# A two-layer streaming encoder: the order of work at two stage entries, and the place of one conditioning product

## The chip, the core and the metric

The kernel runs on one core of a Trainium2 chip. The metric is the device time of one execution in microseconds. The core has a matrix engine (TensorE, PE in the rows; PEld is its weight load), VectorE (DVE), ScalarE (ACT), GpSimd (POOL) and a queue engine that issues transfers (SyncE, SP).

## The reference

Two layers work on 1024 prompt tokens and 64 sample tokens at width 1024. Each sub-layer is norm, conditioning, product, gated residual. Cut to what matters:

```python
sc = silu(c)
for l in range(2):
    m = (sc @ w_ada[l] + b_ada[l])              # 6 vectors of 1024 for each token group
    sh1, sc1, g1, sh2, sc2, g2 = (m[:, i] for i in range(6))
    hn = rms_norm(x, norm_mix[l]) * (1 + sc1) + sh1
    o = even_mix(hn, ...) if l % 2 == 0 else odd_mix(hn, ...)
    x = x + (1 + g1) * o
    hn = rms_norm(x, norm_ffn[l]) * (1 + sc2) + sh2
    x = x + (1 + g2) * ((silu(hn @ wg) * (hn @ wu)) @ wd)
y = rms_norm(x, final_norm)
```

`even_mix` is stick-breaking attention beside a gated linear recurrence (HGRN), `odd_mix` a Griffin block whose first step is `hn @ w_in` into a gate half and an x half. `rms_norm` needs the sum of the squares of a token over all 1024 features before the token can be scaled. The vector `g2` of layer 0, called the fifth conditioning here (i = 5), is first needed when the feed-forward of layer 0 adds its result to x.

## The kernel before

Everything is kept with features on the 128 partitions and tokens along the free axis: NT = 1088 tokens, eight tiles `x[k]`. A float32 product is made of three passes: each operand is split into a rounded high part and the rest (`split`, L98: the cast on ACT, the subtraction of L100 on DVE or POOL), and PE adds hi·hi, hi·lo and lo·hi. For most products the tokens go in chunks `CH` of 384, 384 and 320.

The stages follow one another in the span: the first norm and product to 94 us; the even layer to 840 us, in which attention and HGRN interleave with the input projection (`gemm`, L129, its weights loaded by `load_in`, L1080); output projection and second norm to 908 us; `up_half(0)` to 1374 us; `down_half(0)` to 1642 us; the entry of the odd layer, that is its first norm and the products with the first x and gate columns, to 1692 us; the odd layer's loop to 2060 us; `up_half(1)` to 2514 us; `down_half(1)` and the final norm to 2800 us.

What sets the order. A scheduler simulates the engines and orders each engine's instructions by priority: `later()` lowers the priority, `soon()` raises it. The wrappers `oV`, `oS`, `oG` and `oPE` keep their instructions in program order instead; `V`, `S`, `G`, `PE` leave them to the scheduler. Each engine then runs its list strictly in order.

**The conditioning.** A vector of `m` for 128 features needs 1024 products for each of the two token groups. There are two forms. `mods_dve` (L190) multiplies a 128x1024 tile of the transposed weights by silu(c) held in two tiles `cbc`: for each group one DVE instruction that multiplies and accumulates, or, with `shared`, for the second group a POOL multiplication (L193) and an ACT accumulation (L194). The other form runs on PE: `load_in` (L1080) takes, once its 24 DVE units are done, one tile of `ada5` at a time through eight products into a bank and a copy to `mods` (L1096 and L1097). Before, the fifth conditioning of layer 0 is made in this second form, under `later()`, in the even layer.

**The seven-product stage.** `up_half` (L425) forms gate and up products of the feed-forward for 20 blocks f = 2 to 21 with seven products of half size in place of eight. Block f has products into the accumulators X, Y, Z, W, X, Z, W, each with 24 matmuls of 128x272; after each product a use runs: n1, n6, p7, n5, n2, p4, p3. `weights(f)` makes seven split weight tiles (`wh` by ACT, `wl` by POOL) out of four raw ones and of sums on DVE (`s`, `wu`, `wg`). The token operands are made once, in `sums` (L467): ACT adds the shift to eight x tiles, DVE forms 16 differences (L477 to L480), and ACT and DVE split 16 halves into T1 to T4. One untransformed block f = 1 runs ahead of them.

`Ada` (L399) does conditioning in the shadow of these blocks: a unit in n1 (two DVE instructions), one in n5 (shared form), and for f below 8 a third one in n2 (shared form). `up_half(0)` does 40 units of layer 1, `up_half(1)` the eight of the gate of layer 1. `load_cbc` (L183) makes the tiles `cbc` by a sigmoid on ACT and a product on DVE (L187).

**The odd entry.** `down_half(0)` calls `after(ci)` when the tokens of chunk ci are final. `use` (L1205) there runs `stats(ci)` for chunks 0 and 1: `norm_stats` (L251) squares the eight x slices (ACT), adds them (DVE), sums over partitions on PE, takes the power on POOL (L234) and spreads it on PE (L241); then `norm_apply` (L267) scales (DVE), shifts (ACT) and splits (ACT, and POOL for five of eight tiles, DVE for three) into h. `stats(2)` is called after the products of chunk 0 (24 matmuls with `wx0`, 24 with `wg0`) with all its PE steps in program order.

## Time and profile before

| | us |
|---|---|
| median of 3 runs | 2803.64 (2800.59 to 2804.72) |
| the profiled execution | 2801.73 |
| its span | 2800.0 |
| PE busy in the span | 2616.5 |
| DVE, ACT, POOL busy | 1855.6, 1022.0, 1180.6 |
| mean granted clock of PE | 0.963 of full |

The profiled execution is 1.73 us longer than its span and 1.91 us under the median. PE is the engine that works most; time in which PE waits, or runs at the lower of its two clock levels (0.5 of full), is what a change of order can touch. A row of the windows view gives a stretch, its length, the busy time and number of instructions of PE, PEld, DVE, ACT and POOL, the granted clock, the share of the DMA engines and the GB/s. A row of the timeline gives a start, a duration, engine, line and operation, output and inputs, size and count, and in brackets the idle time before it and what ended that.

### The profile page before, as it was taken

The numbers are of one execution on the slowest core, as the hardware profiler recorded it, in microseconds if no ns is written. First come the engines' busy times: TensorE is split into PE (matmuls) and PEld (weight loads), VectorE is DVE, ScalarE is ACT, GpSimd is POOL, SyncE is SP. The second block draws the span as 40 slices with busy tenths as digits, with TensorE's granted clock in tenths as the row PEclk, the third lists the DMA queues.
The fourth block names the chain that finished last, engine by engine and source line by source line (L and its number), as shares of the span: only waits on it lengthen the run. The fifth ranks groups of instructions, "written<-read, shape, count | busy, mean of one in ns | idle before, by whom it ended". The sixth has DMA issues, their size and how long they took to land. (4 is left out here: it accounts for less than half of the span.)

```text
span 2800.0 us, 44597 instructions
## 1 busy us (share of the span) xinstructions
PE 2616.5 (93%) x17680; PEld 2553.8 (91%) x17680; DVE 1855.6 (66%) x2850; ACT 1022.0 (36%) x1862; POOL 1180.6 (42%) x795
## 2 busy tenths in 40 slices
PE   5898999999988899999999979998889999999998
PEld 5898989998878899999999979988889999999997
DVE  8768763667897778876465575658877444446556
ACT  3225343354454533333221146564363222222112
POOL 6446443455441477765322233444126444433112
PEclk8999989899999999999999989999999999999999
DMA  6232111113112344443432101121223222226211
GB/s 240 91 113 92 46 58 55 57 53 130 57 50 103 108 141 133 130 138 108 152 130 94 62 16 59 68 74 63 98 74 122 70 81 83 70 92 219 89 61 64
DMA packets 99663, 261.98 MB, mean 94 GB/s; under 512 B 16640, under 2 KB 36096, under 8 KB 99456
## 3 DMA queue, kind: packets, MB, share of 16 engines
q1 hardware_dynamic: 99168, 258.03, 27.7%
q8 instruction: 139, 2.28, 0.3%
q10 hardware_dynamic: 288, 1.11, 0.1%
q14 instruction: 68, 0.56, 0.1%
HBM read 208.41 MB, written 50.69 MB: 93 GB/s over the span
## 5 line engine op out<-in xcount | busy, mean ns | idle before, releaser
L100 POOL TENSOR_TENSOR w_lo<-w_raw,w_hi 128x1024 fp32r<-128x1024 f32 x92 | 237.3, 2586 | 533.9 <-ACT w_hi L99 484.6
L100 POOL TENSOR_TENSOR wl<-wg,wh 128x512 fp32r<-128x512 f32 x164 | 225.4, 1381 | 375.6 <-ACT wh L99 333.6
L507 PE MATMUL accZ<-op,wh 128*128 128x272 f32 x1280 | 245.5, 289 | 5.8 <-DVE tmp L51 5.7
L507 PE MATMUL accW<-op,wh 128*128 128x272 f32 x1280 | 244.3, 288 | 0.0
L507 PE MATMUL accX<-op,wh 128*128 128x272 f32 x1280 | 243.5, 288 | 0.0
L99 ACT CAST w_hi<-w_raw 128x1024 fp32r<-128x1024 f32 x90 | 93.2, 1050 | 362.3 <-PE ps_mm L313 253.5
L129 PE MATMUL ps_mm<-h_hi,w_hi 128*128 128x384 f32 (+1 forms) x624 | 213.2, 342 | 2.8 <-ACT w_hi L99 1.3
L129 PE MATMUL ps_mm<-h_hi,w_lo 128*128 128x384 f32 (+1 forms) x624 | 212.4, 342 | 2.0 <-POOL w_lo L100 2.0
L129 PE MATMUL ps_mm<-h_lo,w_hi 128*128 128x384 f32 (+1 forms) x624 | 212.0, 340 | 0.0
L507 PEld LDWEIGHTS accZ<-op,wh 128*128 128x128 f32 x1280 | 201.1, 188 | 7.6 <-DVE tmp L51 6.2
L99 ACT CAST wh<-wg 128x512 fp32r<-128x512 f32 x160 | 97.5, 619 | 296.9 <-DVE wg L51 191.4
L318 DVE SCALAR_TENSOR_TENSOR x<-ps_mm,mods,x 128x384 f32<-128x384 f32 (+4 forms) x334 | 152.2, 480 | 75.1 <-PE ps_mm L313 73.9
L507 PEld LDWEIGHTS accW<-op,wh 128*128 128x128 f32 x1280 | 201.3, 188 | 0.0
L507 PEld LDWEIGHTS accX<-op,wh 128*128 128x128 f32 x1280 | 200.9, 188 | 0.0
L507 PE MATMUL accZ<-op,wl 128*128 128x272 f32 x640 | 184.6, 288 | 1.0 <-POOL wl L100 1.0
L507 PE MATMUL accX<-op,wl 128*128 128x272 f32 x640 | 184.5, 288 | 0.0
L507 PE MATMUL accW<-op,wl 128*128 128x272 f32 x640 | 184.5, 288 | 0.0
L318 DVE SCALAR_TENSOR_TENSOR x<-ps_t,mods,x 128x384 f32<-128x384 f32 (+3 forms) x220 | 107.1, 504 | 87.9 <-PE ps_t L313 87.9
L51 DVE SCALAR_TENSOR_TENSOR tmp<-hid,cbc 128x1024 f32<-128x1024 f32 x68 | 132.0, 1941 | 21.6 <-ACT tmp L194 20.9
L100 POOL TENSOR_TENSOR wl<-wu,wh 128x512 fp32r<-128x512 f32 x84 | 131.7, 1569 | 27.9 <-ACT wh L99 27.3
L507 PE MATMUL accY<-op,wh 128*128 128x272 f32 x640 | 124.7, 292 | 16.1 <-ACT wh L99 16.1
L318 DVE SCALAR_TENSOR_TENSOR x<-ps_z,mods,x 128x384 f32<-128x384 f32 (+2 forms) x198 | 91.3, 485 | 61.4 <-PE ps_z L313 60.6
(485 smaller groups left out, 8066.1 us busy)
## 6 DMA issues: line engine op xcount, KB each, us to landing
hid<-in_adaT SPq DMA_DIRECT2D x48, 512.0 KB, 3.9
w_raw<-in_wd SPq DMA_DIRECT2D x44, 512.0 KB, 3.8
hid_dram<-tmp SPq DMA_DIRECT2D x80, 272.0 KB, 2.1
hid_lo<-hid_dram SPq DMA_DIRECT2D x40, 544.0 KB, 4.7
wg<-in_wg SPq DMA_DIRECT2D x42, 512.0 KB, 3.9
wu<-in_wu SPq DMA_DIRECT2D x42, 512.0 KB, 3.6
w_raw<-in_w_in_even SPq DMA_DIRECT2D x28, 512.0 KB, 3.7
w_raw<-in_adaT SPq DMA_DIRECT2D x24, 512.0 KB, 3.6
```

The lines of the kernel that those rows point to most:

```text
L51: return lambda *a, **k: self.tc.keep_in_program_order(f(*a, **k))
L99: S.copy(hi, src)
L100: (lo_eng or G).tensor_sub(lo, src, hi.bitcast(F32))
L129: PE.matmul(ps[:, :n], a[:, k * P:(k + 1) * P], b[:, c0:c0 + n], start=(i == 0), stop=(i == last))
L318: V.scalar_tensor_tensor(x[m][:, r0:r0 + rn], ps[:, r0 - c0:r0 - c0 + rn], gate[:, m, b:b + 1], x[m][:, r0:r0 + rn], ALU.mult, ALU.add)
L507: PE.matmul(acc[:, j, :Q], a[:, k * P:(k + 1) * P], op[k][:, b, c], start=(start == 1 and i == 0), stop=(i == 11), skip_group_check=True)
```

## The change

Four edits.

1. **Odd entry.** `norm_stats` is split into `norm_squares` (squares and their sum) and the rest. `after(ci)` makes the squares of chunk ci ahead of the scaling of chunk ci-1, the squares of chunk 2 ahead of the scaling of chunk 1. The sum of chunk 2 over partitions and the power come after the 48 products of chunk 0, its spread and scaling after the first 24 of chunk 1.
2. **The fifth conditioning.** The PE form in `load_in` is gone with its 64 calls, its eight loads of `ada5` and its copies. `Ada` of `up_half(0)` gets 48 units in place of 40, and the blocks with a third unit are f = 2 to 15 in place of f = 2 to 7; in `up_half(1)` no block has a third unit, where f = 2 to 4 had one.
3. **`load_cbc`** uses silu on ACT alone; the sigmoid and the two DVE products of L187 go, and with the function the changes between two ACT tables.
4. **`sums`** adds the shift in the order 0, 4, 1, 5, 2, 6, 3, 7, does 12 of the 16 differences first, then the splits in the order of the products that use them (T2, T3, T1, T4), and keeps all of it in program order.

```diff
...
-    def load_cbc(ts, sg):
+    def load_cbc(ts):
         for v in range(2):
             dma(ts[v], I["cT2"][v:v + 1, :].partition_broadcast(P))
-            S.activation(sg, ts[v], AF.Sigmoid)
-            V.tensor_mul(ts[v], ts[v], sg)
+            S.activation(ts[v], ts[v], AF.Silu)
         return ts
...
     def norm_stats(chunk, x, tmp, PE=PE, pool=(1, 2), S=S):
+        acc = norm_squares(chunk, x, tmp, pool, S)
+        return inv_rms([lambda: acc], chunk[1], 1.0 / 1024, PE)
+
+    def norm_squares(chunk, x, tmp, pool=(), S=S):
...
-        return inv_rms([lambda: acc], n, 1.0 / 1024, PE)
+        return acc
...
         def __init__(self, todo):
-            self.todo = [(i, j) for i in todo for j in range(KD)]
+            self.todo = [(l, i, j) for l, i in todo for j in range(KD)]
+            self.thrice = 2 + max(0, len(self.todo) - 2 * (FF - 5))
...
-            self.cb = load_cbc([pool.tile([P, 1024], F32, name="cbc", tag="cbc", bufs=2) for v in range(2)],
-                               raw())
+            self.cb = load_cbc([pool.tile([P, 1024], F32, name="cbc", tag="cbc", bufs=2) for v in range(2)])
...
-                dma(raw, I["adaT"][48 + i * KD + j])
...
-                mods_dve(1, i * KD + j, self.cb, raw, self.junk, shared, oV)
+                l, i, j, raw = self.ready.pop(0)
+                mods_dve(l, i * KD + j, self.cb, raw, self.junk, shared, oV)
                 if j == KD - 1:
-                    finish_mods(1, i)
+                    finish_mods(l, i)
     def up_half(l, plain, x, t_tag, op_tag, ada):
         B = B12, B11, B21, B22 = plain[0]
...
             def sums():
-                for k in range(KD):
+                for k in (0, 4, 1, 5, 2, 6, 3, 7):
                     for r0, rn, b in rng(0, NT):
                         v = x[k][:, r0:r0 + rn]
                         oS.activation(v, v, AF.Identity, bias=mods[l][:, 3 * KD + k, b:b + 1])
                 T1, T3, T4 = ([halves(fp.tile([P, NT], F32R, name="op", tag=t, bufs=4)) for _ in range(4)]
                               for t in ("t1", "t3", "t4"))
+                T2 = []
+                part = lambda k: (x[k][:, :HT], x[k][:, HT:], x[k + 4][:, :HT], x[k + 4][:, HT:])
                 for k in range(4):
-                    a, b, c, d = x[k][:, :HT], x[k][:, HT:], x[k + 4][:, :HT], x[k + 4][:, HT:]
-                    V.tensor_sub(d, b, d)
-                    V.tensor_sub(b, b, a)
-                    V.tensor_sub(a, a, d)
-                    V.tensor_sub(c, c, a)
-                    split(d, T3[k][:, 0, :], T3[k][:, 1, :], V, S=oS)
-                    split(b, T1[k][:, 0, :], T1[k][:, 1, :], V, S=oS)
-                    split(c, T4[k][:, 0, :], T4[k][:, 1, :], V, S=oS)
-                T2 = []
+                    a, b, c, d = part(k)
+                    oV.tensor_sub(d, b, d)
+                    oV.tensor_sub(b, b, a)
+                    oV.tensor_sub(a, a, d)
                 for k in range(4):
                     T2.append(halves(u(op_tag, F32R, "op")))
-                    split(x[k][:, :HT], T2[k][:, 0, :], T2[k][:, 1, :], V)
+                    split(part(k)[0], T2[k][:, 0, :], T2[k][:, 1, :], oV, S=oS)
+                for k in range(4):
+                    split(part(k)[3], T3[k][:, 0, :], T3[k][:, 1, :], oV, S=oS)
+                for k in range(4):
+                    split(part(k)[1], T1[k][:, 0, :], T1[k][:, 1, :], oV, S=oS)
+                for k in range(4):
+                    a, b, c, d = part(k)
+                    oV.tensor_sub(c, c, a)
+                    split(c, T4[k][:, 0, :], T4[k][:, 1, :], oV, S=oS)
                 return B11, T2, T3, T1, B21, T4, B22
             stage["open"].close()
...
                     def n2():
                         S.activation(g, x_, AF.Silu)
-                        if f < 8:
+                        if f < ada.thrice:
                             ada.one(True)
                             ada.fetch(1)
...
                 yield
         todo = [(i, j) for i in (2, 3, 4) for j in range(KD)]
-        todo_pe = list(range(KD))
         def load_in(t):
             w = load_w(wi[t])
...
                     mods_dve(0, i * KD + j, cb, raw, lambda: mp.tile([P, 1024], BF16, name="junk", tag="junk"))
                     if j == KD - 1:
                         finish_mods(0, i)
-                if not todo and todo_pe:
-                    j = todo_pe.pop(0)
-                    raw = raw_tile()
-                    dma(raw, I["ada5"][j])
-                    ps = bank("o")
-                    for e in range(KD):
-                        PE.matmul(ps[:, :2], raw[:, e * P:(e + 1) * P], sc[:, e, :], start=(e == 0), stop=(e == KD - 1))
-                    V.tensor_copy(mods[0][:, 5 * KD + j, :], ps[:, :2])
-                    if j == KD - 1:
-                        finish_mods(0, 5)
             return w
         def out_group(g, after=None, chunks=CH):
...
     stage["open"] = banks_open
-    got = up_half(0, plain, x, "B", "A", Ada(range(5)))
+    got = up_half(0, plain, x, "B", "A", Ada([(0, 5)] + [(1, i) for i in range(5)]))
     xg_open = ExitStack()
     xg = xg_open.enter_context(phase_pool("xg"))
...
         ntmp = lambda: fp.tile([P, 384], F32, name="ntmp", tag="ntmp", bufs=13)
         h = []
-        def use(x):
-            rs = {}
-
-            def stats(ci, PE=PE):
-                rs[ci] = norm_stats(CH[ci], x, ntmp, PE, (), oS if ci == 2 else S)
-                if not h:
-                    h.extend(new_h("B", "C"))
-                for k in range(KD):
-                    norm_apply(ci, k, x, rs[ci], 1, 0, h, ntmp)
-
-            use.stats = stats
+        accs, rs = {}, {}
+
+        def squares(ci):
+            accs[ci] = norm_squares(CH[ci], x, ntmp, (), oS if ci == 2 else S)
+
+        def apply(ci):
+            if not h:
+                h.extend(new_h("B", "C"))
+            for k in range(KD):
+                norm_apply(ci, k, x, rs[ci], 1, 0, h, ntmp)
+
+
+        def use(x_):
+            nonlocal x
+            x = x_
             with later():
                 decay_consts()
-            return None, lambda ci: stats(ci) if ci < 2 else None, None
-
-        x = down_half(0, fp, "A", "B", got, use)
+
+            def after(ci):
+                squares(ci)
+                if ci == 0:
+                    rs[0] = inv_rms([lambda: accs[0]], CH[0][1], 1.0 / 1024)
+                elif ci == 1:
+                    apply(0)
+                    rs[1] = inv_rms([lambda: accs[1]], CH[1][1], 1.0 / 1024)
+                else:
+                    apply(1)
+
+            return None, after, None
+
+        down_half(0, fp, "A", "B", got, use)
         wio = I["w_in_odd"]
         OS = 1027
...
         for ci in range(3):
             hold = lambda to: lambda *a: outs.append((to, a))
             gemm_chunk(wx0, h, hold(x_to(xg0, oS)), ci, range(KD), ("mm", "t", "mm")[ci], oPE)
+            if ci == 1:
+                rs[2] = rms_spread(r2, CH[2][1], oPE)
+                apply(2)
             gemm_chunk(wg0, h, hold(g_to(xg0, oS)), ci, range(KD), ("z", "z", "t")[ci], oPE)
             if ci == 0:
-                use.stats(2, oPE)
+                r2 = rms_pow(rms_sum([lambda: accs[2]], CH[2][1], oPE), CH[2][1], 1.0 / 1024)
             with soon():
                 while outs:
                     to, a = outs.pop(0)
...
     xg_open.close()
-    got = up_half(1, plain, x, "A", "B", Ada((5,)))
+    got = up_half(1, plain, x, "A", "B", Ada([(1, 5)]))
     with phase_pool("ffn1") as fp:
         stage["w"] = fp
         layout(fp, ("hid", 2 * NT, 2), ("late", 2 * NT, 1), ("wd_lo", 1024, 6), ("w_raw", 1024, 2),
```

In the lists below, one row is an instruction or several alike: line, operation, output and inputs, tile. L51 stands for all instructions that a wrapper issues in program order; numbers behind a name tell buffers apart.

VectorE at the start of `up_half(0)`, before, up to the weight sum `wg` from which the second product's weights are split (`x` are differences, `op<-x,op` low parts of splits, `hid` the block f = 1, the last row is the first conditioning unit):

```order
L386 TENSOR_TENSOR hid_8640<-hid_8640,accZ 128x272
L100 TENSOR_TENSOR op<-x,op 128x544
L480 TENSOR_TENSOR x<-x 128x544
L100 TENSOR_TENSOR op<-x,op 128x544
L386 TENSOR_TENSOR hid_8640<-hid_8640,accW 128x272
L100 TENSOR_TENSOR op<-x,op 128x544 x2
L51 TENSOR_TENSOR wu<-wg,wu 128x512
L100 TENSOR_TENSOR op<-x,op 128x544 x2
L51 TENSOR_TENSOR wg<-s_8871,wg 128x512
L51 SCALAR_TENSOR_TENSOR tmp,mods_70<-hid_8863,cbc 128x1024 x2
```

The same engine and place after:

```order
L51 TENSOR_TENSOR op<-x,op 128x544 x9
L51 TENSOR_TENSOR x<-x 128x544
L389 TENSOR_TENSOR hid_8542<-hid_8542,accZ 128x272
L389 TENSOR_TENSOR hid_8542<-hid_8542,accW 128x272
L51 TENSOR_TENSOR s_8770<-wu 128x512
L51 TENSOR_TENSOR op<-x,op 128x544
L51 TENSOR_TENSOR x<-x 128x544
L51 TENSOR_TENSOR wu<-wg,wu 128x512
L51 TENSOR_TENSOR wg<-s_8770,wg 128x512
L51 SCALAR_TENSOR_TENSOR tmp,mods_69<-hid_8762,cbc 128x1024
```

Of the 16 differences 14 and of the 16 low parts 13 stand ahead of `wg` now, where all 32 did; three of the low parts and two differences come behind it, and the two products of L187 are gone.

VectorE in block f = 8 of `up_half(0)`, before (`tmp,mods` is a conditioning unit, `tmp<-accZ,tmp` at the sixth product the sum that frees Z):

```order
L51 TENSOR_TENSOR tmp<-accW,tmp 128x544
L51 SCALAR_TENSOR_TENSOR tmp,mods_70<-hid_10239,cbc 128x1024
L51 TENSOR_TENSOR s_10428<-wu 128x512
L51 TENSOR_TENSOR wu<-wg,wu 128x512
L51 TENSOR_TENSOR wg<-s_10428,wg 128x512
L51 TENSOR_TENSOR tmp<-accZ,tmp 128x544
L51 TENSOR_TENSOR tmp<-tmp 128x544
```

The same block after:

```order
L51 TENSOR_TENSOR tmp<-accW,tmp 128x544
L51 SCALAR_TENSOR_TENSOR tmp,mods_70<-hid_10138,cbc 128x1024
L51 TENSOR_TENSOR s_10327<-wu 128x512
L51 TENSOR_TENSOR wu<-wg,wu 128x512
L51 TENSOR_TENSOR wg<-s_10327,wg 128x512
L51 SCALAR_TENSOR_TENSOR tmp,mods_70<-hid_10238,cbc 128x1024
L51 TENSOR_TENSOR tmp<-accZ,tmp 128x544
L51 TENSOR_TENSOR tmp<-tmp 128x544
```

A third unit stands between the weight sum and the sum that frees Z, as it stood in blocks 2 to 7 before.

TensorE in the odd entry, before, at the end of chunk 0's products (`ones,ntmp` is the sum of squares over partitions, `ident,r` the spread, `ps_t` the first products of chunk 1):

```order
L51 MATMUL ps_z<-h_hi,w_hi 128x384
L225 MATMUL ps_o<-ones,ntmp 128x1 x3
L51 MATMUL ps_z<-h_lo,w_hi 128x384
L51 MATMUL ps_z<-h_hi,w_lo 128x384
L51 MATMUL ps_z<-h_hi,w_hi 128x384
L51 MATMUL ps_z<-h_lo,w_hi 128x384
L51 MATMUL ps_z<-h_hi,w_lo 128x384
L241 MATMUL ps_o<-ident,r_15861 128x128 x3
L51 MATMUL ps_o<-ones,ntmp 128x1 x3
L51 MATMUL ps_o<-ident,r_16067 128x128 x3
L51 MATMUL ps_t<-h_hi,w_hi 128x384
```

The sum of chunk 2 after, behind the last of chunk 0's products:

```order
L51 MATMUL ps_z<-h_hi,w_hi 128x384
L51 MATMUL ps_z<-h_lo,w_hi 128x384
L51 MATMUL ps_z<-h_hi,w_lo 128x384
L51 MATMUL ps_o<-ones,ntmp 128x1 x3
L51 MATMUL ps_t<-h_hi,w_hi 128x384
L51 MATMUL ps_t<-h_lo,w_hi 128x384
```

and the spread of chunk 2 after, between the x and the gate products of chunk 1:

```order
L51 MATMUL ps_t<-h_hi,w_hi 128x384
L51 MATMUL ps_t<-h_lo,w_hi 128x384
L51 MATMUL ps_t<-h_hi,w_lo 128x384
L51 MATMUL ps_o<-ident,r_16008 128x128 x3
L51 MATMUL ps_z<-h_hi,w_hi 128x384
L51 MATMUL ps_z<-h_lo,w_hi 128x384
```

The sum and the spread of chunk 2 stood next to each other ahead of all products of chunk 1; now 24 products of chunk 1 stand between them. The sum of chunk 1, which stood 43 products into chunk 0, stands in the last products of `down_half(0)`, and its spread 19 products into chunk 0.

## Rows read from the trace of the kernel before

**Rows 1.** The page: busy us, share of the span and instructions of each engine

```profile
PE 2616.5 (93%) x17680; PEld 2553.8 (91%) x17680; DVE 1855.6 (66%) x2850; ACT 1022.0 (36%) x1862; POOL 1180.6 (42%) x795
```

**Rows 2.** Windows, line 1096 alone: us, PE busy (x), PEld busy (x), clock, DMA share, GB/s

```profile
392.00:409.50 17.50, 6.91 (x32) 7.29 (x32) 0.51 0.31 99
409.50:438.00 28.50, 3.74 (x32) 3.96 (x32) 1.00 0.10 31
492.00:508.50 16.50, 2.93 (x13) 3.12 (x13) 0.50 0.38 121
340.00:560.00 220.00, 20.03 (x128) 21.04 (x128) 0.88 0.18 56
```

**Rows 3.** Timeline of PE in the even layer: start, us, instruction

```profile
395.63 3.51 PE L1096 MATMUL ps_o<-sc,w_raw 128*128 128x2 f32 x16
399.01 1.52 PE L904 MATMUL ps_t<-ident,be 128*128 128x128 f32 x6
```

**Rows 4.** Waits of PE, 340 to 560 us: us in total, times, longest

```profile
PE ps_t L904 <- DVE vs L855: 2.5, 1, 2.5
```

**Rows 5.** Windows at the start of up_half(0), all engines

```profile
936.40:944.70 8.30, 0.35 (x4) 0.13 (x2) 8.30 (x14) 3.54 (x8) 0.02 (x1) 0.83 0.45 148
944.70:948.70 4.00, 4.00 (x16) 3.88 (x17) 2.58 (x4) 1.98 (x4) 4.00 (x3) 0.50 0.42 116
```

**Rows 6.** Timelines of ACT and DVE at the same place

```profile
910.30 8.83 ACT L51 ACTIVATE x<-x,mods 128x1024 f32<-128x1024 f32 x13
943.99 0.62 ACT L99 CAST wh<-wg 128x512 fp32r<-128x512 f32 x1 [4.08 <-DVE wg L51]
916.83 0.72 DVE L477 TENSOR_TENSOR x<-x 128x544 f32<-128x544 f32 x1 [9.09 <-ACT x L51]
926.68 1.22 DVE L187 TENSOR_TENSOR cbc<-cbc,hid 128x1024 f32<-128x1024 f32 x1
943.28 0.68 DVE L51 TENSOR_TENSOR wg<-s,wg 128x512 f32<-128x512 f32 x1
```

**Rows 7.** Timeline of PE at the start of up_half(1)

```profile
2091.68 0.82 PE L507 MATMUL accY<-op,wh 128*128 128x272 f32 x2 [7.95 <-ACT wh L99]
```

**Rows 8.** Windows of blocks: f = 4, f = 5, f = 5 to 8, f = 9; up_half(1) f = 5

```profile
985.88:1006.93 21.05, 21.05 (x171) 21.05 (x170) 14.58 (x16) 7.88 (x15) 16.07 (x9) 1.00 0.47 152
1006.93:1030.68 23.75, 22.06 (x171) 21.30 (x169) 20.49 (x23) 6.75 (x13) 17.07 (x9) 1.00 0.41 136
1006.93:1098.51 91.58, 86.51 (x675) 84.81 (x674) 76.08 (x81) 29.89 (x55) 67.43 (x36) 1.00 0.44 140
1110.53:1131.58 21.05, 21.05 (x171) 21.05 (x169) 19.00 (x19) 7.62 (x14) 14.92 (x10) 1.00 0.50 150
2153.83:2176.68 22.85, 21.88 (x171) 21.23 (x169) 13.12 (x18) 7.17 (x13) 14.12 (x10) 1.00 0.23 78
```

**Rows 9.** Timelines of DVE and POOL, third units of f = 3 and f = 7, and between

```profile
987.03 2.10 DVE L51 SCALAR_TENSOR_TENSOR tmp<-hid,cbc 128x1024 f32<-128x1024 f32 x1 [2.26 <-ACT tmp L194]
1079.08 2.11 DVE L51 SCALAR_TENSOR_TENSOR tmp<-hid,cbc 128x1024 f32<-128x1024 f32 x1 [2.26 <-ACT tmp L194]
1007.86 0.69 DVE L51 TENSOR_TENSOR wu<-wg,wu 128x512 f32<-128x512 f32 x1
1050.24 2.71 DVE L51 TENSOR_TENSOR wu<-wg,wu 128x512 f32<-128x512 f32 x1
1049.68 2.72 POOL L193 TENSOR_TENSOR hid<-hid,cbc 128x1024 f32<-128x1024 f32 x1 [1.23 <-issue]
```

**Rows 10.** Windows of the odd entry

```profile
1657.90:1670.50 12.60, 0.03 (x1) 0.00 (x0) 12.36 (x17) 8.07 (x18) 6.99 (x6) 0.67 0.00 0
1670.50:1679.20 8.70, 7.41 (x27) 7.35 (x28) 4.40 (x16) 3.73 (x12) 2.59 (x3) 0.50 0.00 0
```

**Rows 11.** Timelines of PE and POOL there

```profile
1670.55 1.41 PE L51 MATMUL ps_o<-ones,ntmp 128*128 128x1 f32 x6 [12.62 <-DVE ntmp L263]
1663.02 6.11 POOL L100 TENSOR_TENSOR h_lo<-ntmp,h_hi 128x384 fp32r<-128x384 f32 x5 [0.43 <-ACT h_hi L99]
```

7 lines of the change are left out of this document (3 added, 4 removed).

## The prediction

> **What bounds the kernel now.** I read the totals first: PE is busy 93% of the span, no other engine over 66% [rows 1]. So time goes down where PE has less to do, waits less or runs at full clock, and it goes up where an edit makes PE wait. Then, stage by stage, the windows and the waits of PE in the four places that the diff touches. In the even layer PE is nearly gapless, but a part of what it does is the fifth conditioning, 128 tiny matmuls, partly at half clock [rows 2]. At the start of each `up_half` PE stands still for some 8 us and runs 4 us at half clock behind it [rows 5, 7]. In blocks 5 to 8 of `up_half(0)` it waits for the DVE sum that frees accumulator Z, and blocks with two units run without a gap [rows 8]. In the odd entry it stands still for 12.6 us and then runs at half clock for 8.7 us [rows 10, 11].
>
> **a) The fifth conditioning leaves PE.** The trace has 128 matmuls of line 1096, 20.0 us of busy time in all: 32 take 6.91 us and 13 take 2.93 us at half clock (0.22 us each), 32 take 3.74 us at full clock (0.12 us each) [rows 2]. A run of them overlaps what follows it by 0.13 us (395.63 + 3.51 against 399.01 [rows 3]); with some ten runs that is 1.3 us, so 18.7 us of PE's time go. Is that on the path? PE's longest wait in the stretch is 2.5 us [rows 4], so the stage is bound by PE, with waits that some of these matmuls may cover. The stretches around them are the ones at half clock, 17.5 and 16.5 us long [rows 2]: there PE's work is thin, 128x2 outputs among it, and the scheduler of the new kernel has projection matmuls of 128x384 to put in these places. If a fifth of the 34 us at half clock came back to full, that is 34 x 0.2 / 2 = 3.4 us more. I take -22. Upper end: all but the half of them covered waits, -8. Lower end: half of the 34 us comes back, 8.5, and with the ordering a little better, -34. The eight loads move from the even layer to `up_half(0)`, where the DMA engines are busy 0.50 of a block at most [rows 8]; cost nothing. The eight copies of L1097 were on a DVE with slack.
>
> **b) Start of up_half(0).** PE waits 936.4 to 944.7 for the weights of the second product: the wait is for ACT's cast at 943.99, that for DVE's `wg` at 943.28, and DVE has worked off its list without a gap since 916.83 [rows 5, 6]. Ahead of `wg` stood 40 instructions. In the new list 2 differences and 3 low parts come behind it, 5 x 0.64 = 3.2 us, and the two products of L187 are gone, 2 x 1.2 = 2.4 us [rows 6]: 5.6 us. It can also begin earlier: before, the first difference waited for the shifts of tiles 0 to 4 (13 ACT instructions take 8.83 us, so 1.3 us a tile [rows 6]); now for tiles 0 and 4, some 3.8 us less. That gain isn't kept whole, since the later differences wait for the later tiles, and the sum for block f = 1 cannot be earlier than PE's last product of that block. I put `wg` at 937.5, the cast behind it at 937.9 and PE's second product at 938.6: 2.2 us of the wait stay, 6.0 go, and 2.0 us for the 4 us at half clock [rows 5], as the stretch of rest ahead of it is so much shorter. That is 8 us for PE at that place. But in `up_half(0)` the blocks behind it run at DVE's pace (c), and DVE is only some 5.6 us ahead of before by then. **-5.6** here, bounds 0 and -8.
>
> **c) A third unit in blocks 8 to 15.** Each is one DVE instruction (2.10 us when POOL works beside it), a POOL pass of 2.72 us and an ACT accumulation, and it stands ahead of the sum that frees Z. What such a block costs can be read from the six that had it: in blocks 2 to 4 nothing is lost (block 4 takes 21.05 us, PE without a gap), as DVE has slack from before; from then on DVE, whose third units follow one another in (1079.08 - 987.03) / 4 = 23.0 us [rows 9], sets the pace. The four blocks 5 to 8 take 91.58 us where four without waits take 84.2 [rows 8]: 7.4 us. In a block with two units DVE is busy 19.00 of 21.05 us [rows 8], so two units just fit and a third does not. In the new kernel the loop at 23.0 us goes on for 8 more blocks: 8 x 1.94 = **+15.5**. Bounds: 8 x 1 = +8 if the new start leaves DVE that slack for longer, and 8 x (23.75 - 21.05) = +21.6 at the worst block seen [rows 8].
>
> A row shows why DVE is so slow here: the sum `wu` takes 2.71 us when POOL's pass runs beside it and 0.69 us without [rows 9]. The Trainium skill, page "SBUF — State Buffer", section "Who interferes with whom", says that a DVE instruction with two SBUF inputs contends with a GpSimd instruction that reads SBUF, and that the later one blocks fully. The trace agrees for `wu` (2.71 beside a pass of 2.72), and by that rule each added pass would block DVE for up to its whole 2.72 us: 8 x 2.72 = +21.8 in place of +15.5, 6 us more in the sum. It speaks against this part of the change.
>
> **d) Odd entry.** PE's wait of 12.62 us is for the last sum of the squares of chunk 2 [rows 11]. DVE was busy 12.36 us of it, with the eight scalings of chunk 1 ahead of those sums [rows 10]. In the new order the squares of chunk 2 come ahead of these scalings, and the sum over partitions finds its input ready. So the wait goes, with 1.3 us of gaps and 7.41 / 2 = 3.7 us of half clock behind it [rows 10]: 12.6 + 1.3 + 3.7 = 17.6 at most. What is late next: the products of chunk 1 need the low parts that POOL makes, five in 6.11 us, the last of them at 1669.1 [rows 11], some 12 us behind the spread of chunk 1. That spread stands now 19 products into chunk 0, near 1648, and squares of chunk 2 (eight on ACT, seven sums on DVE) lie in between: chunk 1 is ready near 1662, when PE has been done with chunk 0 for some 5 us. The power of chunk 2 sits behind those five POOL instructions, its spread near 1663; the same 12 us lead to 1675, and some 4 us of products are left then: the entry ends near 1679 in place of 1692. **-13**, bounds -6 (the clock falls again in the wait that is left) and -17.
>
> **e) up_half(1).** The same start: PE waited 7.95 us [rows 7], and no blocks at DVE's pace follow. -8 as in b). And block 5, which took 22.85 us with a third unit before it [rows 8], takes 21.05 without: -1 to -1.8. **-9**, bounds -5 and -11.
>
> Sum: -22 - 5.6 + 15.5 - 13 - 9 = -34. Against the profiled execution of 2801.73 that is 2767.6; it was 1.9 under the median, so 2769.5 against the median, **2770**.
>
> **Rivals.**
> R1: the conditioning on PE only covered waits of the attention. For it: they were last in priority, so the scheduler put them where nothing else was ready, and waits remain beside them [rows 4]. Against it: the longest of these waits is 2.5 us [rows 4], so that PE's other work had little to be covered. Term a is then -4: 2770 + 18 = 2788.
> R2: the third unit stays hidden, since the earlier start gives DVE enough slack and ACT has fewer table changes. For it: block 4 with its third unit lost nothing [rows 8]. Against it: DVE's pace of 23.0 us is longer than the block, so slack of 6 us is used up in three blocks. Term c is 0: 2770 - 15.5 = 2754.
> R3, slower: the clock falls in the blocks with a third unit. In the odd entry and at the start of the stage a long stop was followed by half clock [rows 5, 10]; against it, in blocks 5 to 8 the clock stayed at 1.00 although PE stopped in them [rows 8]. If stops grow in 14 such blocks to where the clock falls, each costs the 2.7 us of the worst block and 2.0 us at half clock [rows 5, 8]: 14 x 4.7 - 7.4 = +58 in place of +15.5, and the sum is +9: 2813. It decides if the added units let the stop before the second Z product grow until the granted clock of such a block reads below 1.00.
> R4: the edits do not reach the chip as written, because the scheduler puts the even layer in another order and opens two new stops there like the one of b) (8.2 and 2.0 us each): a is -18.7 + 20.4 = +2, and the time 2770 + 24 = 2794.
>
> **How the numbers follow.** My forecast has a chance of 0.68, R1 0.13, R2 0.07, R3 0.05, R4 0.07. The unknown bounds (a by +14 and -12, c by +6 and -7.5, d by +7 and -4, b and e by some 5) add to about 17 either way if they don't all fall together: 2753 to 2787. R1 lies at its upper edge, R4 above, R2 at its lower edge; from 2750 to 2794 no more than 2 in 10 is left out. A difference of 0.2%, 5.6 us, is about what a measurement of this kernel can tell from no change: faster is below 2798, slower above 2809. Faster holds the forecast, R1, R2 and most of R4: 0.89. Slower is R3 and a corner of R4: 0.05. Between them 0.06.
>
> **What would show it.** In the profile after: no matmuls of line 1096's kind and a higher clock between 340 and 560 us (a); a stop of some 2 us in place of 8.2 at the first Y product of either `up_half` and full clock behind it (b, e); blocks 9 to 16 of `up_half(0)` near 23 us and at clock 1.00 (c); the stop of 12.6 us gone, with one of some 5 us behind chunk 0, and the stage over within 37 us (d). The forecast is wrong if the even layer is as long as before (a), if blocks with a third unit run at half clock (c), or if chunk 1 waits in the odd entry as long as chunk 2 did (d).

## The result, and the profile after

The changed kernel takes 2758.05 us (median of 4 runs, 2757.01 to 2763.7) beside 2802.78 us for the kernel before: ratio 0.9849, 95% interval 0.9831 to 0.9868, so 42 us less by the ratio. The forecast was 2770 us with a range of 2750 to 2794. Measured again later, beside another kernel below, the ratio was 0.9872 (0.9853 to 0.9891).

The table sets the two profiled executions side by side. A stage begins with PE's first matmul of it, the odd entry with the last matmul of `down_half(0)`; each difference is that of two such stretches. "Forecast" is the term of the prediction.

| stage | before, us | after, us | difference | forecast |
|---|---|---|---|---|
| start and first product | 94.3 | 93.7 | -0.6 | 0 |
| even layer to norm (a) | 814.6 | 775.7 | -38.9 | -22 |
| up_half(0) (b, c) | 470.0 | 484.3 | +14.3 | +9.9 |
| down_half(0) | 263.4 | 265.3 | +1.9 | 0 |
| odd entry (d) | 51.4 | 35.5 | -15.9 | -13 |
| odd layer's loop | 362.2 | 365.2 | +3.0 | 0 |
| up_half(1) (e) | 463.4 | 454.1 | -9.3 | -9 |
| down_half(1), final norm | 280.7 | 282.9 | +2.2 | 0 |
| span | 2800.0 | 2756.8 | -43.2 | -34 |

The page of the kernel after: the busy time of each engine, and the clock granted to PE in 40 slices.

```profile
PE 2591.9 (94%) x17552; PEld 2528.9 (92%) x17552; DVE 1871.9 (68%) x2856; ACT 1017.3 (37%) x1868; POOL 1201.2 (44%) x802
PEclk9999999999999999999999999999999999999998
```

PE has 128 matmuls less, as many as line 1096 had [rows 1, 2], and is busy 24.6 us less; the span is shorter by 43 us, so more than work was saved.

Windows of the kernel after (stretch, length, busy time and instructions of PE, PEld, DVE, ACT, POOL, clock, DMA share, GB/s): the even layer's middle, the first 3.4 us behind the stop at the start of `up_half(0)`, two of its block lengths (from one second Z product to the next, block 8 to 9 and 9 to 10), the clock behind the stop in the second of them, and the odd entry in three parts.

```profile
340.00:520.00 180.00, 174.72 (x1178) 166.53 (x1177) 116.43 (x176) 76.93 (x179) 86.47 (x70) 0.98 0.14 41
337.35:519.95 182.60, 177.32 (x1193) 169.13 (x1193) 119.08 (x178) 77.20 (x180) 88.96 (x72) 0.98 0.13 41
899.10:902.50 3.40, 3.31 (x20) 2.66 (x21) 3.40 (x4) 2.03 (x4) 3.38 (x3) 1.00 0.36 135
1049.61:1072.28 22.67, 21.56 (x169) 21.20 (x169) 18.58 (x19) 7.72 (x15) 16.79 (x10) 1.00 0.44 139
1072.28:1100.46 28.18, 23.20 (x169) 23.00 (x170) 19.78 (x25) 7.43 (x14) 16.66 (x11) 0.88 0.44 144
1089.60:1093.00 3.40, 3.40 (x15) 3.40 (x16) 2.68 (x4) 0.66 (x1) 0.68 (x1) 0.50 0.72 242
1619.05:1630.00 10.95, 9.86 (x57) 8.98 (x55) 10.95 (x27) 9.58 (x23) 6.77 (x7) 1.00 0.01 2
1630.00:1642.00 12.00, 10.25 (x54) 10.28 (x55) 5.70 (x16) 7.21 (x17) 5.61 (x7) 0.86 0.00 0
1642.00:1654.50 12.50, 9.36 (x56) 8.09 (x54) 3.78 (x11) 7.66 (x23) 5.29 (x8) 1.00 0.08 17
```

The first two rows answer [rows 2]: the work that lay between 340 and 560 us lies, by the count of the other matmuls, between 337.35 and 519.95 now, and the clock of the stretch rose from 0.88 to 0.98. The fourth row is near what the prediction expected of a block with a third unit, 22.7 us at full clock. The fifth is one that it did not expect.

The timeline of PE at the stops that answer [rows 5], [rows 8] and [rows 11] (the first Y product of `up_half(0)`, the first Z product of its block 10, the sum of chunk 2 in the odd entry):

```profile
899.10 0.51 PE L515 MATMUL accY<-op,wh 128*128 128x272 f32 x2 [1.86 <-ACT wh L99]
1089.57 0.79 PE L515 MATMUL accZ<-op,wh 128*128 128x272 f32 x2 [4.98 <-DVE tmp L51]
1631.75 0.80 PE L51 MATMUL ps_o<-ones,ntmp 128*128 128x1 f32 x6 [1.82 <-DVE ntmp L266]
```

The first stop, some 8 us before, is 1.9 us now, and the third, 12.6 us before, 1.8 us. The second is new: this Z product has to wait until DVE has read what block 9 left in Z. Its cause, in the units of block 9 on POOL, ACT and DVE:

```profile
1084.85 2.34 POOL L192 TENSOR_TENSOR hid<-hid,cbc 128x1024 f32<-128x1024 f32 x1
1087.23 1.06 ACT L193 ACTIVATE tmp<-hid 128x1024 f32<-128x1024 f32 x1 [4.58 <-POOL hid L192]
1088.41 0.18 DVE L173 TENSOR_TENSOR mods<-mods,vec 128x16 f32<-128x16 f32 x1 [4.64 <-ACT tmp L193]
1088.71 0.72 DVE L51 TENSOR_TENSOR tmp<-accZ,tmp 128x544 f32<-128x544 f32 x1
```

With eight units more, the 24th unit, the last of a vector, falls on the third call of block 9. The addition that closes a vector (L173) follows it on DVE at once and needs its ACT accumulation, which needs the POOL pass: DVE waits 4.64 us, and behind it in DVE's list stands the sum that frees Z. PE stops for 5 us and then runs 3.4 us at half clock.

### The profile page after: what moved, and what is told of

Same layout as the page of the kernel before. It is cut to its first block, busy times and chain, and to the rows that moved or that the text cites. A ratio compares the mean times of both kernels' runs of the same rounds, so it can differ in the third digit from the quotient of the medians.

```text
span 2756.8 us, 44383 instructions
## 1 busy us (share of the span) xinstructions
PE 2591.9 (94%) x17552; PEld 2528.9 (92%) x17552; DVE 1871.9 (68%) x2856; ACT 1017.3 (37%) x1868; POOL 1201.2 (44%) x802
## 3 DMA queue, kind: packets, MB, share of 16 engines
q8 instruction: 138, 2.26, 0.4%
## 5 line engine op out<-in xcount | busy, mean ns | idle before, releaser
L515 PEld LDWEIGHTS accZ<-op,wh 128*128 128x128 f32 x1280 | 201.9, 189 | 22.7 <-DVE tmp L51 14.3
L51 DVE SCALAR_TENSOR_TENSOR tmp<-hid,cbc 128x1024 f32<-128x1024 f32 x77 | 151.4, 1966 | 36.0 <-ACT tmp L193 35.3
```

The source lines that it names most:

```text
L51: return lambda *a, **k: self.tc.keep_in_program_order(f(*a, **k))
L515: PE.matmul(acc[:, j, :Q], a[:, k * P:(k + 1) * P], op[k][:, b, c], start=(start == 1 and i == 0), stop=(i == 11), skip_group_check=True)
```

## The experiments

Each kernel was timed beside the kernel before; its own runs give the ratio. Stage times are from its profiled execution. Such stages scatter: the even layer has PE's instructions in the same order in the kernel before and in two of the kernels below (the new sums alone, the odd entry alone), and took 814.6, 808.8 and 804.5 us, by the places where the clock fell. A stage's difference between two profiles is therefore read with some us of doubt.

### What the even layer gained

**The conditioning product taken out of the kernel before, nothing put in its place.**

```diff
-        todo_pe = list(range(KD))
+        todo_pe = []
+        V.memset(mods[0][:, 5 * KD:6 * KD, :], 1.0)
```

> The kernel before without its 128 matmuls of the fifth conditioning and their eight loads and copies; nothing takes their place (the gate of the first feed-forward is left at one, so this part of the computation is left out). Theory T1: these matmuls, with 2 columns each, cost their own 18.7 us and pull the granted clock down for the projection work around them; with them gone the stretch from 340 us on is 39 to 40 us shorter and its clock goes from 0.88 to 0.98, whatever the other edits do: 2763 us. Rival T2: the even layer gained its extra 20 us from the other edits of the change; then this kernel gains the 18.7 us of work alone, 2784 us, and the clock stays near 0.88 to 0.9.

Measured: 2764.87 us, ratio 0.9868 (0.9843 to 0.9893), 37 us less by the ratio, 34 by the medians. The even layer takes 776.3 us, the stages with the other edits are as before (up_half(0) 470.0, odd entry 51.2, up_half(1) 463.4). The window of its even layer's middle is the one of the kernel after, to the hundredth of a us of PE's busy time:

```profile
340.00:520.00 180.00, 174.72 (x1176) 166.54 (x1175) 116.91 (x176) 76.56 (x178) 86.89 (x71) 0.98 0.14 41
```

So the whole gain of the stage is that of taking the conditioning out of it; the other edits have no part in it.

**The same matmuls issued twice.**

```diff
-                    for e in range(KD):
+                    for e in [*range(KD)] * 2:
                         PE.matmul(ps[:, :2], raw[:, e * P:(e + 1) * P], sc[:, e, :], ...
```

> The kernel before with each matmul of the fifth conditioning issued twice (256 of 128x2 in place of 128; the result is the same). T1: 18 to 20 us for the work and again a lower clock around it, so +25 to +45 us and a mean clock below 0.88 in the stretch from 340 us on. Rival T3: the matmuls cost only their own time, and the clock of that stretch was low for another reason: +14 (all at full clock) to +20 us and the clock as before.

Measured: 2835.86 us, ratio 1.013 (1.0101 to 1.0158), 36 us more; the even layer takes 842.5 us, 28 us more than in the profile of before. The stretch from 340 us on runs at 0.84:

```profile
340.00:590.00 250.00, 241.23 (x1463) 232.51 (x1463) 125.62 (x194) 83.62 (x188) 89.46 (x72) 0.84 0.16 50
```

Each set of 128 adds about the same, 34 to 37 us (the intervals of the two ratios are 30 to 44 and 28 to 44 us) against some 19 us of work; the clock goes 0.98, 0.88, 0.84 with none, one and two sets. T1 holds against T3: the cost is more than the matmuls' own time. One profile does not fix the clock: in the two kernels below with PE's order of before, the new sums alone and the odd entry alone, the stretch reads 0.89 and 0.93.

```profile
340.00:560.00 220.00, 214.00 (x1348) 203.84 (x1347) 126.54 (x195) 83.48 (x189) 93.10 (x74) 0.89 0.18 56
340.00:560.00 220.00, 210.93 (x1381) 200.97 (x1381) 127.91 (x198) 85.72 (x193) 93.00 (x73) 0.93 0.19 56
```

**Wide matmuls in their places.**

```diff
-                    raw = raw_tile()
-                    dma(raw, I["ada5"][j])
                     ps = bank("o")
-                    for e in range(KD):
-                        PE.matmul(ps[:, :2], raw[:, e * P:(e + 1) * P], sc[:, e, :], ...
+                    for e in range(2 * KD):
+                        o = e % KD * P
+                        PE.matmul(ps[:, :256], w[0][:, o:o + P], w[0][:, :256], ...
```

> The kernel before with each of the 128 matmuls of 128x2 in float32 replaced by one of 128x256 in the rounded format, at the same places, out of the weight tile just loaded (the fifth conditioning is left out, its values are not the reference's; the eight loads are gone too). About the same time on the engine, some 0.12 us each, 15 us in all, but many columns. T1: it is the few columns that lower the clock: the stretch from 340 us on runs at 0.96 or more and the time is 39 - 15 = 24 us below before, 2779 us. Rival T3: the places and the order lower the clock, or the time is theirs whatever their width: within 6 us of before, clock 0.88 to 0.90.

Measured: 2787.59 us, ratio 0.9953 (0.9938 to 0.9968), 13 us less. First row: these matmuls alone; second: the stretch.

```profile
340.00:550.00 210.00, 19.92 (x128) 18.41 (x128) 0.93 0.13 40
340.00:550.00 210.00, 200.93 (x1332) 192.06 (x1331) 130.12 (x197) 83.94 (x191) 83.65 (x72) 0.93 0.13 40
```

They are busy 19.9 us, as the conditioning's were (20.03 us [rows 2]), so the difference of 13 us is not one of work. But it is half of what T1 in its sharp form asked for, 24 us. The clock of this profile is 0.93, under the 0.96 that was expected; above the 0.88 of before, but no higher than the 0.93 that one profile with the 128x2 matmuls had, so here the timing decides and not the clock. A part of the cost belongs to the small outputs, a part remains with 128x256.

**Two columns again, without the loads.** As the last, with `ps[:, :2]` and `w[0][:, :2]`.

> As the kernel with 128x256 matmuls in place of the conditioning, but with 2 columns again, in the rounded format and out of the weight tile just loaded (the fifth conditioning is left out; the eight loads are gone). T1: few columns lower the clock, loads or not: the clock of the stretch from 340 us on stays near 0.88 to 0.92 and, since a matmul in this format is shorter, the time is 5 to 20 us below before. Rival T4: what held the stage back were the eight tiles loaded for these matmuls, which take the two buffers of the weight loads; then this kernel is as fast as the one without them, some 30 us or more below before, clock 0.96 or more.

Measured: 2804.61 us, ratio 1.0019 (1.0008 to 1.003), 5 us more than before. The matmuls alone, and the stretch:

```profile
340.00:560.00 220.00, 21.25 (x128) 21.56 (x128) 0.89 0.12 37
340.00:560.00 220.00, 215.35 (x1365) 205.57 (x1364) 125.58 (x195) 85.22 (x191) 90.56 (x73) 0.89 0.12 37
```

Without the eight loads nothing is gained: T4 falls. That these matmuls would be shorter in the rounded format was wrong too, they are busy 21.25 us. Between the last two kernels only the columns differ, with nearly the same time on the engine (1.3 us apart), and 17 us lie between them. Why this kernel is 5 us slower than before is not shown.

### What up_half(0) paid

**The changed kernel without the eight units.**

```diff
+        V.memset(mods[0][:, 5 * KD:6 * KD, :], 1.0)
...
-    got = up_half(0, plain, x, "B", "A", Ada([(0, 5)] + [(1, i) for i in range(5)]))
+    got = up_half(0, plain, x, "B", "A", Ada([(1, i) for i in range(5)]))
```

> The changed kernel without the eight conditioning units of the fifth vector in up_half(0), so that its third units stand in blocks 2 to 7 again (the gate of the first feed-forward is left at one: this part of the computation is left out). Theory: the eight further blocks at DVE's pace cost 15.5 us and the stop of 5.3 us in block 9 with its clock 6 to 7 us more; up_half(0) goes from 484.3 us to 462 to 465 us, and 5 to 8 us below the 470.0 us of before, which is the price of the new start. Rival: the new start gains nothing in up_half(0), since blocks 3 to 8 are bound by DVE anyway; then 468 to 470 us.

Measured: 2746.1 us, ratio 0.9811 (0.9782 to 0.9839); up_half(0) 468.8 us. The eight units cost 484.3 - 468.8 = 15.5 us. But this is 1.2 us under before, not 5 to 8: for the new start in this stage the rival is right.

**The closing addition later.**

```diff
+            self.made = []
...
                 if j == KD - 1:
-                    finish_mods(l, i)
+                    self.made.append((l, i))
+
+        def finish(self):
+            while self.made:
+                finish_mods(*self.made.pop(0))
...
                     if f == FF - 3:
...
+                        ada.finish()
...
                     def n1():
                         S.copy(t, x_)
                         ada.one(False)
+                        ada.finish()
```

> The changed kernel, with the addition that ends a vector of the conditioning (L170, on DVE) issued after the first unit of the next block and not right behind the unit whose accumulation on ACT it needs. Theory: in block 9 DVE no longer waits 4.6 us for that accumulation ahead of the sum that frees Z; PE's stop of 5.3 us there becomes one of some 1.4 us like its neighbours', and blocks 5 and 13, where the addition stood behind the unit of n5, lose 1 to 2 us each: up_half(0) 475 to 479 us in place of 484.3, 2749 to 2753 us in all. Rival: DVE's list is full, so the time comes back later in the same blocks: 483 to 485 us, no change.

Measured: 2753.7 us, ratio 0.9842 (0.982 to 0.9865), beside the 0.9849 of the changed kernel no difference that the timing can tell. In the profile the stop behind block 9 is gone, the blocks there take 22.7 to 22.8 us, and up_half(0) takes 480.2 us, 4.2 us less, somewhat under the 5 to 9 us expected. The other 11.4 us of the eight units are the pace of blocks 9 to 16, most of them at 22.6 to 22.9 us.

**The changed kernel again**, beside the next one.

> The changed kernel once more, beside the next one on the same chip: 2756 to 2764 us. up_half(0) 484 us by its stop of 5.3 us in block 9 if that stop comes from the order of DVE's list, as in the first profile; if it was an accident of one execution, 476 to 479 us.

Measured: 2762.11 us, ratio 0.9872 (0.9853 to 0.9891); up_half(0) 485.4 us, and PE's wait behind block 9 is there again:

```profile
PE accZ L515 <- DVE tmp L51: 6.1, 2, 5.0
```

(Waits of PE from 1060 to 1120 us: us in all, times, longest.) It comes from the order.

**The third unit behind the sum that frees Z.** On top of the later closing addition, the call moves from n2 to the end of p4:

```diff
                     def n2():
                         S.activation(g, x_, AF.Silu)
-                        if f < ada.thrice:
-                            ada.one(True)
-                            ada.fetch(1)
...
                     def p4():
                         oV.tensor_add(hA, z_, t)
                         oV.tensor_mul(hA, hA, g)
                         dma(hid_dram[f][:, :HT], hid[:, :HT])
+                        if f < ada.thrice:
+                            ada.one(True)
+                            ada.fetch(1)
```

> The changed kernel with the closing addition of a vector after the next block's first unit, and with the third unit of a block called at the end of p4 in place of n2, so behind the sum and the product that follow the sixth product; the number of units in a block is the same. Theory: a block with three units takes 22.7 us not because DVE is full (it is busy 37.1 of 45.3 us in two such blocks) but because of the order: DVE waits 2.3 us there for ACT's accumulation, which writes the same scratch tile, ahead of the sum that frees Z. Behind that sum the wait is over before the unit comes, and the blocks take 21.05 to 21.6 us: up_half(0) 462 to 470 us, 2738 to 2747 us in all. Rival, by which I reckoned in the forecast: DVE's throughput with POOL beside it sets the pace, the third unit costs its time wherever it stands, and the blocks stay at 22.4 to 22.9 us: up_half(0) 478 to 482 us, 2750 to 2757 us.

Measured: 2753.83 us, ratio 0.9839 (0.9823 to 0.9856); up_half(0) 478.3 us, blocks still mostly at 22.6 to 23.1 us. My theory fell. A block of it, DVE's instructions around the third unit there, and its POOL pass:

```profile
1048.92:1071.57 22.65, 21.35 (x169) 21.13 (x169) 20.74 (x19) 7.73 (x15) 16.77 (x10) 1.00 0.46 141
1052.52 2.71 DVE L51 TENSOR_TENSOR wu<-wg,wu 128x512 f32<-128x512 f32 x1
1058.55 2.31 DVE L51 SCALAR_TENSOR_TENSOR tmp<-hid,cbc 128x1024 f32<-128x1024 f32 x1
1062.23 2.73 DVE L51 TENSOR_TENSOR tmp<-tmp 128x544 f32<-128x544 f32 x1 [0.73 <-ACT tmp L578]
1061.98 2.40 POOL L192 TENSOR_TENSOR hid<-hid,cbc 128x1024 f32<-128x1024 f32 x1
```

The wait for ACT ahead of the third unit [rows 9] is gone, but the instructions became longer: the product `tmp<-tmp` that follows takes 2.73 us beside the second POOL pass. DVE is busy 20.74 of 22.65 us in place of 18.58 in the changed kernel's block above.

**All units in the DVE form.** With the later closing addition, and `ada.one(False)` for `ada.one(True)` in n2 and in n5: no POOL passes, no ACT accumulations.

> The changed kernel with the closing addition after the next block's first unit, as before, and with every conditioning unit of both up_half stages in the form of two DVE instructions: no POOL pass of L192 and no accumulation on ACT; one more DVE instruction of 1.2 us (2.1 beside POOL) in its place. Theory: DVE and POOL hold each other up. The run with the third unit behind Z had no wait of DVE for ACT any more and the same 22.7 us: in its place DVE instructions took 1.9 to 2.7 us beside POOL where they take 0.7 to 1.2 alone. If the two exclude each other, a pass of 2.3 us costs both of them that time, and its DVE form 1.2 us: two passes in a block less are -2.2 us, 22.7 - 2.2 = 20.5, so a three-unit block fits into PE's 21.05 us: up_half(0) 458 to 465 us, 2733 to 2743 us in all. Rival: DVE is the bound by its own instructions, and two more of 2.1 us make a three-unit block 23 to 26 us: up_half(0) 485 to 520 us, above the changed kernel.

Measured: 2730.77 us, ratio 0.9748 (0.9725 to 0.9771), 70 us less than before and 27 us less than the changed kernel by its ratio of 0.9849, 35 by its second, 0.9872. up_half(0) takes 457.3 us, and every three-unit block from f = 3 on 21.05 us. A stretch of that length, and two of DVE's instructions there and in the next block:

```profile
1095.50:1116.55 21.05, 21.05 (x170) 21.05 (x169) 17.77 (x24) 5.86 (x11) 11.07 (x8) 1.00 0.50 153
1101.93 0.69 DVE L51 TENSOR_TENSOR wu<-wg,wu 128x512 f32<-128x512 f32 x1
1119.16 0.72 DVE L51 TENSOR_TENSOR tmp<-accW,tmp 128x544 f32<-128x544 f32 x1 [2.06 <-PE accW L520]
```

DVE does 24 instructions where it did 19 in the changed kernel's block above, and is busy less: 17.77 us for 18.58. The sum `wu` is back at 0.69 us, and DVE waits 2.06 us for PE: it has slack now.

**Only the third unit in the DVE form.** As the last, but n5 keeps `ada.one(True)`.

> The same with the DVE form for the third unit alone; the unit in n5 keeps its POOL pass. Theory of exclusion: one pass of 2.3 us less and one DVE instruction of 1.2 us more, 22.7 - 1.1 = 21.6 us for a block: up_half(0) 466 to 473 us, 2741 to 2750 us in all. Rival (DVE bound by its own instructions): 23 to 25 us a block, up_half(0) 483 to 505 us.

Measured: 2761.05 us, ratio 0.9857 (0.9833 to 0.9881); up_half(0) 484.6 us, three-unit blocks mostly 23.1 to 23.4 us: nothing gained, and my sum of pass and instruction was wrong for this kernel. What it keeps is the pass in n5 (third row), and its two prices on DVE:

```profile
1166.31 2.72 DVE L51 TENSOR_TENSOR wu<-wg,wu 128x512 f32<-128x512 f32 x1
1172.08 2.11 DVE L51 SCALAR_TENSOR_TENSOR tmp<-hid,cbc 128x1024 f32<-128x1024 f32 x1 [2.26 <-ACT tmp L193]
1165.69 2.79 POOL L192 TENSOR_TENSOR hid<-hid,cbc 128x1024 f32<-128x1024 f32 x1 [2.37 <-DVE tmp L51]
```

2.72 - 0.69 = 2.0 us by which the pass holds up `wu`, and 2.26 us of waiting for the ACT accumulation that goes through the same scratch tile: 4.3 us against the 1.2 to 2.3 us of one more DVE instruction. That single pass, with its accumulation on ACT, decides between 23.2 and 21.05 us; the two were not taken apart.

### The two entries

**Only the new sums and the silu, in the kernel before.** The bodies of `sums` and `load_cbc` as in the change.

> The kernel before with only the new order in sums and the silu of load_cbc. Theory: PE's stop of 8.2 us at the first Y product of either up_half becomes one of some 2.2 us at full clock; up_half(1) is 8 us shorter (455.3 us), up_half(0) 5 to 6 us (464.5 us), the rest as before: 13 to 14 us less in all, 2787 against a before of 2800. Rival: all of up_half(1)'s gain of 9.3 us comes from its missing third units and the stop is paid later: up_half(1) 462 us or more.

Measured: 2793.68 us, ratio 0.9987 (0.9976 to 0.9998), only some 4 us less. PE's stop is 1.9 us long at either start, near the 2.2 forecast. But the stages gained 1.7 us (up_half(0) 468.3) and 2.8 us (up_half(1) 460.6). From the start of the stage to the end of block 2 it is 51.6 against 56.0 us in up_half(0) and 51.7 against 55.8 in up_half(1), 4.3 and 4.1 us less, and some of that is lost in later blocks. A window behind the stop at the start of up_half(1):

```profile
2083.75:2087.05 3.30, 3.27 (x15) 3.09 (x14) 3.30 (x3) 1.27 (x3) 3.30 (x3) 0.50 0.03 12
```

Some 3.3 us run at half clock here, where in the changed kernel's first profile the like stop in up_half(0) was followed by full clock (899.10:902.50, above). From the start of up_half(0) to the end of block 2, in the kernel before and in the first and the second profile of the changed kernel:

```profile
908.88:964.83 55.95, 47.90 (x360) 47.34 (x361) 39.91 (x55) 37.40 (x60) 21.55 (x15) 0.94 0.28 94
869.41:918.46 49.05, 47.00 (x361) 45.72 (x362) 41.51 (x51) 29.39 (x51) 21.16 (x13) 1.00 0.32 107
870.38:922.01 51.63, 49.66 (x361) 48.69 (x361) 42.29 (x52) 29.50 (x52) 21.12 (x13) 0.93 0.30 102
```

So one kernel has both: the gain at a start is 6.9 us where the clock stays up and 4.3 us where it falls.

**Only the odd entry, in the kernel before.** The bodies of `norm_stats`, `use` and the loop over chunks as in the change.

> The kernel before with only the new order at the odd entry. Theory: the entry takes 35 to 37 us in place of 51.4, all else as before: 14 to 16 us less in all, 2785 against a before of 2800. Rival: a part of the 15.9 us came from elsewhere (the earlier end of the feed-forward, other states of the clock); then 40 us or more.

Measured: 2787.43 us, ratio 0.9961 (0.9949 to 0.9974), 11 us less; the entry takes 35.25 us, at full clock:

```profile
1635.92:1671.17 35.25, 28.25 (x165) 25.67 (x163) 20.46 (x52) 24.49 (x60) 17.67 (x20) 1.00 0.04 7
```

The entry's 16 us belong to this edit alone. The timing gives less, 7 to 14 us by its interval and so under the 14 to 16 expected; where the rest went is not shown. In this profile down_half(0), the odd layer's loop and the last stage take 2.3 to 2.8 us longer each than in that of before. In seven kernels with it the entry took 35.2 to 35.5 us, and 38.2 in the one where the clock fell to 0.87 over it (the changed kernel's second profile).

## Why the prediction was right, point by point

The total holds in part by errors that met: by the table the even layer gave 16.9 us more than forecast and the odd entry 2.9 more, up_half(0) gave 4.4 less, and 6.5 were lost in stages that had no term.

**a) The fifth conditioning: right in sign, mis-sized, -22 for -39.** The 39 is that of two profiles, and the one of before is the longest of its order: the three profiles with the matmuls average 809.3 us, the eight without them 775.1, so some 34 us is the fairer figure, at the lower end of the forecast's bounds. The work was right: 20 us of busy time went. The term that failed is the clock: "If a fifth of the 34 us at half clock came back to full, that is ... 3.4 us more." The window of the kernel before that goes with the 337.35:519.95 of after is:

```profile
340.00:560.00 220.00, 211.01 (x1322) 201.18 (x1321) 122.59 (x191) 81.99 (x187) 90.52 (x72) 0.88 0.18 56
```

220 us at 0.88 hold 2 x 0.12 x 220 = 53 us at half clock, 182.6 us at 0.98 hold 7 us. The stretch is 37.4 us shorter: 20.0 us of the matmuls' busy time (some 4.6 of it by the clock, 45 of them at 0.22 in place of 0.12 us), 13.7 us by which the other matmuls are busy less (191.0 to 177.3), and 3.7 us of idle time (9.0 to 5.3). So the clock is worth up to 18 us, where the forecast had 3.4. I saw that the stretches at half clock were those around these matmuls and that their outputs were thin, and yet counted 34 us at half clock, where the 0.88 of [rows 2] already holds 53, and let only a fifth of them come back. That the columns matter is shown by the two kernels that differ in nothing else (17 us); that all of the clock's part is due to them is not, since 128x256 in the same places brought back only a part.

**b) The start of up_half: right in the stop, too large in the gain.** Forecast 2.2 us of stop, measured 1.9; the list of DVE was the bound, as read. The step that failed is "2.0 us for the 4 us at half clock": the clock still falls behind the shorter stop in several executions. The edit gives 4.1 to 6.9 us at a start, not 8; in the kernel with it alone, in which the clock fell at both, 1.7 us (for -5.6) remain at the end of up_half(0) and 2.8 at that of up_half(1).

**c) A third unit in eight more blocks: right size, 15.5 us for +15.5, by two errors that met.** 11.4 us are the pace, most blocks at 22.7 us and not 23.0; 4.2 us are the stop behind block 9 (5.2 beside the changed kernel's second profile, whose clock fell at the stage's start as it did in the kernel without the stop), which I had not seen although the trace of before showed the same thing in small. Block 5 there, with 23.75 us the worst [rows 8], begins while DVE stands at a closing addition:

```profile
1006.99 0.18 DVE L173 TENSOR_TENSOR mods<-mods,vec 128x16 f32<-128x16 f32 x1 [3.74 <-ACT tmp L194]
```

That DVE's pace bounds such blocks was right. Its reason was not a third unit as such: with all units on DVE alone three fit in 21.05 us. It is the POOL pass and its ACT accumulation. The Trainium skill, page "SBUF — State Buffer", section "Who interferes with whom", states that a DVE instruction with two SBUF inputs contends with a GpSimd instruction that reads SBUF. The rows agree with it (`wu` 2.7 us beside a pass, 0.69 us without); the price drawn from it, 2.72 us for each added pass, wasn't reached. The moved third unit shows how a wait that is taken out comes back as a longer instruction.

**d) Odd entry: right, -15.9 for -13.** The wait of 12.6 us became 1.8. I expected PE to wait some 5 us for chunk 1's low parts; it doesn't. The scheduler mixed the last sums of chunk 2 (L264, L266) with the scalings of chunk 1 (L276) on DVE, so the 1.8 us that are left are for the last of those sums, with some 3.4 us at half clock behind them, and chunk 1 follows without a stop:

```profile
1627.23 1.65 DVE L276 SCALAR_TENSOR_TENSOR ntmp<-x,scale,ps_o 128x384 f32<-128x384 f32 x3
1628.81 0.62 DVE L266 TENSOR_TENSOR ntmp<-ntmp 128x320 f32<-128x320 f32 x1
1629.35 1.65 DVE L276 SCALAR_TENSOR_TENSOR ntmp<-x,scale,ps_o 128x384 f32<-128x384 f32 x3
1630.92 0.68 DVE L266 TENSOR_TENSOR ntmp<-ntmp 128x320 f32<-128x320 f32 x1
```

**e) up_half(1): -9.3 for -9, partly by luck.** Block 5 gave 1.8 us, as forecast (21.05 for 22.85 us). The start gave 6.6 us and not 8, and that only because no stretch at half clock stands in the first 60 us of the stage in the profile of after. Of the seven profiles with these edits four are like it, 454.1 to 454.8 us; in the three others (the eight units left out, the closing addition later, the third unit behind Z) the clock fell at the start, and they had 456.7 to 457.5 us, 6 to 7 us less than before.

**What was nowhere in the sum:** +6.5 us in stages that the change doesn't touch. Most of it is scatter, in which the profile of before stood at the lower end: in five other kernels with the code of before in these stages (the conditioning left out, doubled, wide, thin; the new sums alone) the odd layer's loop took 364.4 to 366.0 us, beside 362.2 before and 365.2 after, and the last stage 280.7 to 283.2, beside 280.7 and 282.9. down_half(0) took 263.3 to 264.7 there, 263.4 before and 265.3 after.

**The rivals.** R1 is excluded by the first experiment: the conditioning covered next to nothing. R2 did not happen in this kernel, but its outcome, three units at no cost, was reached with the other form of unit. Of R3 one place showed the mechanism, a stop of 5 us and half clock behind it; the other blocks with a third unit stayed at 1.00, as in [rows 8]. R4 did not happen.

**A version that beats both:** the changed kernel with all units in the DVE form and the closing addition later, 2730.77 us.

## What to carry to other kernels

Price a tiny instruction on the matrix engine by the clock of the stretch around it, not only by its duration: look at the granted clock with and without such work, and take the removal's gain from the whole stretch. Where two engines hold each other up, handing half a job to the second engine can cost the first more than the job: compare the long and the short instances of one instruction before splitting work. And when units of work are recounted, look where the step that closes a group of them now falls, and what is queued behind it.

## What the runs showed of the hardware that was not expected

128 matmuls with 2 output columns cost 34 to 37 us where they are busy for 20; with 256 columns in the same places, busy for 19.9, the kernel was 13 us faster, and 17 us faster than with 2 columns in the same format, busy for 21.3. In float32 and in the rounded format the matmuls with 2 columns took nearly the same (20.0 and 21.3 us for 128).

The even layer with one and the same order of PE's instructions took 804.5 to 814.6 us in three profiled executions of three kernels, by where its clock fell; without the thin matmuls it took 771.1 to 777.9 us in eight.
